# Second layer's convolution: taps read from the projection's PSUM bank, with the history columns written in front of it there

## The chip, the core and the metric

The kernel runs on one core of a Trainium2 chip. The metric is the device time of one execution in microseconds, and lower is better. The time before is the median of three runs. One more execution was taken with the hardware profiler, and its own time is given beside its span.

## What is computed

The reference is one inference step of a two-layer streaming encoder, for 1024 prompt frames of a new stream and 64 sample frames of a running one, with shared weights (1088 columns in all, model width 1024). Layer 0 mixes a gated short convolution with banded attention. Layer 1, which the change touches, is a gated DeltaNet of 8 heads. Cut to what matters:

```
def causal_dwconv(u, hist, w):            # width 4 in layer 1
    up = concatenate([hist, u], axis=1)   # 3 columns of history in front
    out = up[:, 0:T] * w[0]
    for j in range(1, 4):
        out = out + up[:, j:j + T] * w[j]
    return out, up[:, -3:]                # and the last 3 inputs, which are an output

def mixer_odd(h, conv_hist, S0, ...):
    p = h @ w_in                          # 1024 -> q | k | v | z | gates
    qkv, new_hist = causal_dwconv(p[q, k, v], conv_hist, conv_w)
    q, k, v = split(silu(qkv))            # 8 heads of 128
    S, o = gated_delta(l2norm(q), l2norm(k), v, g, beta, S0)   # chunks of 64 frames, one after the other
    y = (rmsnorm(o) * silu(z)) @ w_out
```

The prompt starts with a history of zeros, and the sample starts with three given columns.

## The kernel before

Everything is held with features on the 128 partitions and frames along the free dimension. The 1088 frames are cut into three groups, `GROUPS` (L22): 384, 384 and 320 columns. The third group holds the last 256 prompt columns and the 64 sample columns.

**Projection.** `project` (L172) computes one weight tile of 128 output features for one group: 24 matmuls (8 blocks of the contraction, each as three products of high and low parts) accumulate in one PSUM bank, a tile named `pjt` of 128 x 512 fp32 that `bank` (L126) hands out. Six banks serve at the start of layer 1; from its third group on, after `less_banks` (L136), there are two, which take turns. So a projection can begin only when nobody needs what the last but one left in its bank. The program's matmuls are all issued at L119 and its transposes at L124.

**Convolution.** `conv` (L699) takes the finished bank of one group and writes a slice of the tile `kq` (keys and queries of a head pair) or `vt` (values). Per group, ScalarE writes the fourth tap straight from PSUM into the destination (L713), and copies the bank into an SBUF tile `raw` behind three columns of history (L715). VectorE writes the history (L707, L710, L712). The first two taps are VectorE's scalar_tensor_tensor from `raw` (L719). The third is ScalarE's product into `tap` (L721), which GpSimd adds (L722). Then comes the SiLU (L729, or, for the six tiles of the first head pair, a tanh with a correction, L726 and L727). The third group is convolved in two pieces, prompt and sample. `raw` is handed to the next group as `prev`, whose last three columns are its history, and its tails go to HBM (L731, L732).

**Order of the work.** There are 24 such weight tiles, six for each of four head pairs. The first four of the first pair are projected group by group in the loop at L1143, with a small copy `tail` as history (L1163). The other 20 run through `conv_tile` (L735), the three groups of a tile one after the other. TensorE's order is fixed by the program: `Order` (L75) runs generators by rank, and the projection, of lowest rank, gives way after each pair of matmuls within a block; between the last matmul of one projection and the first two of the next nothing is put. Beside the projections run, for each pair and batch of chunks, `prepare` (L855), `substitute` (L918, a forward substitution on GpSimd, L930 and L931, with a trip through HBM on both sides), `join` (L938, which starts with GpSimd's L959 and VectorE's transpose `XT` at L960), `solve` (L1006), `scan` (L1032) and `finish` (L1104). The order on VectorE, ScalarE, GpSimd and the DMA queues is set by a scheduler when the program is built.

**Weights.** When a tile's three groups are done, `drop` (L168) stages another weight tile: ScalarE rounds the high part `whi` (L161) and VectorE subtracts for the low part `wlo` (L162), twice each. Both overwrite the buffer of a tile that was just used.

Of the kernel before, what the change touches and what calls it, by code (L numbers as in the profile page):

```python
# [7 lines left out]
F32 = mybir.dt.float32  # L8
F32R = mybir.dt.float32r
I32 = mybir.dt.int32  # L10
AF = mybir.ActivationFunctionType
ALU = mybir.AluOpType
# [3 lines left out]
P = 128  # L16
# [4 lines left out]
KT = D // P  # L21
GROUPS = ((0, 384), (384, 384), (768, 320))  # L22
GMAX = 384
# [29 lines left out]
P_SCC = 157  # L53
# [54 lines left out]
class Net:  # L108
# [60 lines left out]
        self.held -= 1  # L169
        self.ahead()  # L170

    def project(self, w, ops, n, m=P, ks=range(KT)):  # L172

        ps = self.bank()
        ks = list(ks)
        for k in ks:
            hi, lo = ops[0][k], ops[1][k]
            o = ps[0:m, :n]
            self.mm(o, w[0][:, k, :], hi, k == ks[0], False)
            self.mm(o, w[0][:, k, :], lo, False, False)  # L180
            yield 0
            self.mm(o, w[1][:, k, :], hi, False, k == ks[-1])
        return ps
# [484 lines left out]
    def odd(self):  # L668
        nc, tc, I, O = self.nc, self.tc, self.I, self.O
        act, dve, pool, par, cst = self.act, self.dve, self.pool, self.par, self.cst  # L670
        w_in, mix, order, Dd, od, Sd = I["w_in1"], self.mixd[1], self.order, self.Dd, self.od, self.Sd
        NB = len(BATCHES)
        k1 = self.open("k1")
# [22 lines left out]
        def ch(x):  # L696
            return x.rearrange("p (c t) -> p c t", t=64)

        def conv(ti, dst, g, ps, prev):  # L699
            t0, n = GROUPS[g]  # L700
            half = ti % 8 < 2
            cw = self.cwh[:, ti // 8, 4 * (ti % 8):4 * (ti % 8) + 4] if half else par[:, P_CWC + 4 * ti:P_CWC + 4 * ti + 4]
            cw = [cw[:, j:j + 1] for j in range(4)]
            pieces = [(0, 0, n)] if g < 2 else [(0, 0, 256), (259, 256, 64)]
            raw = k1.tile([P, GMAX + 3], F32, name="raw", tag="raw", bufs=3)
            if g == 0:
                dve.memset(raw[:, 0:3], 0.0)  # L707
            else:
                w = prev.shape[-1]
                dve.tensor_copy(raw[:, 0:3], prev[:, w - 3:w])  # L710
            if g == 2:
                dve.tensor_copy(raw[:, 259:262], par[:, P_SCC + 3 * ti:P_SCC + 3 * ti + 3])  # L712
            act.activation(dst[:, t0 // 64:(t0 + n) // 64, :], ch(ps[:, :n]), AF.Copy, scale=cw[3])  # L713
            for i0, off, m in pieces:
                act.copy(out=raw[:, i0 + 3:i0 + 3 + m], in_=ps[:, off:off + m])  # L715
            for i0, off, m in pieces:
                o = dst[:, (t0 + off) // 64:(t0 + off + m) // 64, :]
                for j in range(2):
                    dve.scalar_tensor_tensor(o, ch(raw[:, i0 + j:i0 + j + m]), cw[j], o, ALU.mult, ALU.add)  # L719
                t = k1.tile([P, GMAX + 3], F32, name="tap", tag="raw", bufs=3)[:, :m]  # L720
                act.activation(t, raw[:, i0 + 2:i0 + 2 + m], AF.Copy, scale=cw[2])  # L721
                pool.tensor_tensor(o, o, ch(t), ALU.add)  # L722
            o = dst[:, t0 // 64:(t0 + n) // 64, :]
            if half:
                th = k1.tile([P, GMAX + 3], F32, name="th", tag="raw", bufs=3)[:, :n]
                act.activation(ch(th), o, AF.Tanh)  # L726
                dve.scalar_tensor_tensor(o, ch(th), 1.0, o, ALU.add, ALU.mult)  # L727
            else:
                act.activation(o, o, AF.Silu)  # L729
            if g == 2:  # L730
                nc.scalar.dma_start(O["convC"][ti, 0], raw[:, 256:259])  # L731
                nc.scalar.dma_start(O["convC"][ti, 1], raw[:, 323:326])  # L732
            return raw

        def conv_tile(ti, dst):  # L735
            w = self.take()
            prev = None
            for g, (t0, n) in enumerate(GROUPS):
                ps = yield from self.project(w, self.hops(g), n)
                prev = conv(ti, dst, g, ps, prev)  # L740
            self.drop()

# [8 lines left out]
        def conv_dst(p, i):  # L751
            q = i % 2
            if i < 2:
                return 8 + 2 * p + q, KQ[p][:, 0, :, q, :]
            if i < 4:
                return 2 * p + q, KQ[p][:, 1, :, q, :]
            return 16 + 2 * p + q, V[p][:, :, q, :]
# [92 lines left out]
        def zeroed():  # L850
            for name, w in (("Cb", 32), ("BD", P)):
                Z[name] = self.kp.tile([P, NBM, w], F32, name=name)
                pool.memset(Z[name], 0.0)
# [287 lines left out]
        ws = [self.wba] + [self.take() for _ in range(WBUFS)] + [self.stage(self.queue.pop(0), k1, 0)]  # L1141
        prev = [None] * (WBUFS + 1)
        for g, (t0, n) in enumerate(GROUPS):  # L1143
            yield f"norm0{g}"
            if g == 2:
                self.close("opn")
                self.less_banks()
                self.pg = self.open("pg", space=PSUM)
                self.kp = self.open("k2", "right")
                zeroed()  # L1150
            for i in range(WBUFS + 2):
                if i == 0:
                    ps = yield from self.project(ws[0], self.hops(g), n, m=16)
                    act.copy(out=ba[:, t0:t0 + n], in_=ps[0:16, :n])
                    if g == 2:
                        order.add("gates", 2, gates(ba))
                        order.add("decays", 3, decays(), ["gates"])
                    continue
                ps = yield from self.project(ws[i], self.hops(g), n)
                raw = conv(*conv_dst(0, i - 1), g, ps, prev[i - 1])  # L1160
                if g < 2:
                    prev[i - 1] = k1.tile([P, 3], F32, name="tail", tag="tail", bufs=WBUFS + 2)
                    dve.tensor_copy(prev[i - 1], raw[:, GMAX:GMAX + 3])  # L1163
                elif i <= WBUFS:
                    self.drop()
        for p in range(4):
            if p > 1:
                yield f"scan{NB * (p - 2) + NB - 1}"
            if p:
                new_kq(p)  # L1170
            for i in range(WBUFS + 1 if p == 0 else 0, 6):
                if i == 4:
                    add_pair(p)
                    if p == 1:
                        yield "decays"
                    new_v(p)
                yield from conv_tile(*conv_dst(p, i))
            order.done.add(f"v{p}")
# [93 lines left out]
```

## Time and profile before

| what | value |
|---|---|
| three runs | 1504.11, 1497.92, 1495.92 us |
| median | 1497.92 us |
| the profiled execution's own time | 1498.51 us |
| its span, first to last instruction | 1496.7 us |
| matmul, busy | 1376.2 us (92%) |
| VectorE, busy | 858.7 us (57%) |
| ScalarE, busy | 745.6 us (50%) |
| GpSimd, busy | 402.1 us (27%) |
| granted TensorE clock, mean | 0.973 |

In the profile, PE is TensorE's matmul, PEld its weight load, DVE is VectorE, ACT ScalarE, POOL GpSimd and SP the DMA queue. A timeline row gives the start, the duration, the engine, the source line, the operation, out<-in with the shape, and how many were merged; in brackets stands the idle time of the engine just before and what ended it. Matmuls are pipelined, so a row's duration is longer than the distance to the next row. Layer 1's convolutions run from about 660 to 1216 us.

### The profile page before, as it was taken

Reading aid. Unit: us, or ns where it says so; the run is one execution under the profiler, and the core shown is the slowest. Engines: PE = TensorE matmul, PEld = TensorE weight load, DVE = VectorE, ACT = ScalarE, POOL = GpSimd, SP = SyncE. Lnnn points to the kernel's source line nnn. Section 1 sums busy time; section 2 is a strip of 40 time slices with the busy share of each in tenths; the row PEclk is TensorE's granted clock in tenths of the full one; section 3 lists DMA queues with packets and bytes.
Section 4 is the critical chain, followed back from the end, with each engine's and each line's share of the span. In section 5 each row is a group of like instructions: output and inputs, shape, how many; then the busy total and the mean of one; then the engine's idle time right before and its main releaser. Section 6 shows DMA issues by size and latency. Waiting matters only on the chain. (4 is left out here: it accounts for less than half of the span.)

```text
span 1496.7 us, 28755 instructions
## 1 busy us (share of the span) xinstructions
PE 1376.2 (92%) x10578; PEld 1237.4 (83%) x10578; DVE 858.7 (57%) x2400; ACT 745.6 (50%) x1948; POOL 402.1 (27%) x909
## 2 busy tenths in 40 slices
PE   4899999999999999898876999999989989999995
PEld 3888998999999899887765877778877778888985
DVE  6647237326525755776675667664756665443654
ACT  6544144235325456776655566556555644323642
POOL 4100000000000014432447254452645261410322
PEclk9999999999999999998987999999999999999998
DMA  5231210220211174541332112211211132337454
GB/s 201 83 114 44 77 58 26 87 65 29 74 61 58 44 233 149 180 146 36 94 87 63 31 51 57 42 41 47 67 35 41 37 96 60 99 108 238 154 190 156
DMA packets 114381, 133.15 MB, mean 89 GB/s; under 512 B 35568, under 2 KB 81336, under 8 KB 114240
## 3 DMA queue, kind: packets, MB, share of 16 engines
q1 hardware_dynamic: 82128, 101.86, 22.9%
q10 hardware_dynamic: 32112, 29.45, 6.1%
q8 instruction: 83, 1.36, 0.4%
q14 instruction: 58, 0.48, 0.1%
HBM read 99.91 MB, written 34.51 MB: 90 GB/s over the span
## 5 line engine op out<-in xcount | busy, mean ns | idle before, releaser
L119 PE MATMUL pjt<-hhi,wlo 128*128 128x384 f32 (+1 forms) x1768 | 621.4, 351 | 1.8 <-DVE wlo L162 1.8
L119 PE MATMUL pjt<-hhi,whi 128*128 128x384 f32 (+1 forms) x1768 | 587.5, 332 | 19.7 <-ACT ko L464 4.2
L119 PE MATMUL pjt<-hlo,whi 128*128 128x384 f32 (+1 forms) x1768 | 586.8, 332 | 7.3 <-DVE hlo L215 6.6
L119 PEld LDWEIGHTS pjt<-hhi,whi 128*128 128x128 f32 x1768 | 340.4, 193 | 29.1 <-ACT hhi L214 6.6
L119 PEld LDWEIGHTS pjt<-hhi,wlo 128*128 128x128 f32 x1768 | 340.3, 192 | 26.0 <-issue 12.2
L119 PEld LDWEIGHTS pjt<-hlo,whi 128*128 128x128 f32 x1768 | 339.0, 192 | 10.5 <-DVE hlo L215 8.8
L162 DVE TENSOR_TENSOR wlo<-wf,whi 128x512 fp32r<-128x512 f32 x222 | 155.6, 727 | 138.3 <-ACT whi L161 137.0
L161 ACT CAST whi<-wf 128x512 fp32r<-128x512 f32 x222 | 129.9, 619 | 154.7 <-PE pjt L119 110.9
L544 ACT ACTIVATE pr<-pr,mx 128x640 f32<-128x640 f32 (+5 forms) x72 | 50.9, 706 | 92.7 <-DVE mx L543 92.2
L722 POOL TENSOR_TENSOR kq<-kq,tap 128x384 f32<-128x384 f32 (+1 forms) x64 | 49.7, 784 | 140.5 <-DVE kq L719 99.5
L505 POOL MEMSET bias<- 64x64 f32 x8 | 1.5, 187 | 315.4 <-DMA bias<-Gd 245.0
L345 POOL TENSOR_TENSOR sqa<-sqa,sq 128x384 f32<-128x384 f32 (+1 forms) x36 | 39.7, 1103 | 150.1 <-ACT sq L343 150.0
L541 DVE CUSTOM_DVE_ANT_0 pr<-sc,bias 128x640 f32<-128x640 f32 (+5 forms) x72 | 48.0, 666 | 26.3 <-PE sc L119 22.8
L1093 DVE SCALAR_TENSOR_TENSOR S<-S,egl,su 128x128 f32<-128x128 f32 x128 | 41.1, 343 | 34.9 <-PE su L119 34.3
L930 POOL TENSOR_TENSOR px<-AL 48x14 f32<-48x14 f32 (+6 forms) x168 | 48.6, 289 | 40.0 <-DMA AL<-Sd 31.6
L931 POOL TENSOR_TENSOR AL<-AL,px 48x14 f32<-48x14 f32 (+6 forms) x168 | 52.4, 312 | 8.7
L719 DVE SCALAR_TENSOR_TENSOR kq<-raw,par,kq 128x384 f32<-128x384 f32 (+1 forms) x96 | 48.7, 526 | 9.9 <-ACT raw L715 9.7
L610 POOL TENSOR_TENSOR cvo<-cvo,th 128x384 f32<-128x384 f32 (+1 forms) x12 | 12.0, 999 | 142.6 <-DVE mx L543 113.3
L884 ACT ACTIVATE junk<-tr 128x128 f32<-128x128 f32 x136 | 38.0, 279 | 19.8 <-PE tr L124 16.5
L124 PE MATMUL pt<-cst,pr 128*128 128x128 f32 (+1 forms) x280 | 43.2, 270 | 4.4 <-DVE pr L546 2.9
L119 PE MATMUL pjt<-mhi,whi 128*128 128x384 f32 x128 | 43.5, 340 | 3.1 <-ACT mhi L161 3.1
L119 PE MATMUL pjt<-mlo,whi 128*128 128x384 f32 x128 | 43.7, 342 | 0.3 <-DVE mlo L162 0.3
(240 smaller groups left out, 2344.5 us busy)
## 6 DMA issues: line engine op xcount, KB each, us to landing
wf<-in_w_in SPq DMA_DIRECT2D x128, 256.0 KB, 3.2
wf<-in_w_out SPq DMA_DIRECT2D x96, 256.0 KB, 3.4
mf<-mixd SPq DMA_DIRECT2D x32, 192.0 KB, 3.5
x<-in_x SPq DMA_DIRECT2D x8, 384.0 KB, 5.3
xg<-in_x SPq DMA_DIRECT2D x2, 1536.0 KB
xd<-xg SPq DMA_DIRECT2D x2, 1536.0 KB, 6.9
Dd<-dbuf ACTq DMA_DIRECT2D x16, 192.0 KB, 2.2
od<-o ACTq DMA_DIRECT2D x12, 256.0 KB, 2.5
```

The costliest lines, as they stand in the source:

```text
L119: return self.pe.matmul(out, lhsT=lhsT, rhs=rhs, start=start, stop=stop, **k)
L124: return self.pe.transpose(out, in_, self.ident[0:k, 0:k])
L161: self.act.copy(out=hi, in_=x)
L162: (eng or self.dve).tensor_tensor(lo, x, hi.bitcast(F32), ALU.subtract)
L345: pool.tensor_tensor(acc, acc, sq, ALU.add)
L541: dve.tensor_tensor_reduce(out=cut(pr[0:nq, :nk]), in0=sc[0:nq, :nk // nw, :nw], in1=cut(b["bias"][a][0:nq, j0:j0 + nk]), scale=1.0, scala ...
L544: act.activation(pr[0:nq, :nk], pr[0:nq, :nk], AF.Exp, bias=mx[0:nq, 1:2], scale=1.0, accum_out=mx[0:nq, 2:3])
L719: dve.scalar_tensor_tensor(o, ch(raw[:, i0 + j:i0 + j + m]), cw[j], o, ALU.mult, ALU.add)
L722: pool.tensor_tensor(o, o, ch(t), ALU.add)
L930: pool.tensor_tensor(t, AL[:, j + 1:16, j:j + 1].broadcast_to([lanes, m, w]), x.broadcast_to([lanes, m, w]), ALU.mult)
L931: pool.tensor_tensor(o, o, t, ALU.add)
L1093: dve.scalar_tensor_tensor(Sn[:, q, :], S[:, q, :], egl[:, q, p, c:c + 1], su[q], ALU.mult, ALU.add)
```

## The change

The bank itself now holds the row of inputs. `project` gets an offset, so that layer 1's results stand in columns 4 onward of their bank. `conv` writes the three columns of history into columns 1 to 3 of the same bank and reads all four taps from there: the fourth by ScalarE as before, the other three by VectorE. The copy `raw`, ScalarE's product and GpSimd's addition are gone. For the sample piece VectorE writes the given history over the last three prompt columns in the bank, after the prompt's taps; before that, ScalarE saves both tails to a small tile `ends`, which goes to HBM. What the next group takes as history is now a slice of the bank, `ps[:, n + 1:n + 4]`. In the first loop it is copied to `tail` at once; in `conv_tile` it is read when the next group's `conv` runs.

```diff
-    def project(self, w, ops, n, m=P, ks=range(KT)):
+    def project(self, w, ops, n, m=P, ks=range(KT), off=0):
...
-            o = ps[0:m, :n]
+            o = ps[0:m, off:off + n]
...
-            raw = k1.tile([P, GMAX + 3], F32, name="raw", tag="raw", bufs=3)
+            o = dst[:, t0 // 64:(t0 + n) // 64, :]
+
+            act.activation(o, ch(ps[:, 4:4 + n]), AF.Copy, scale=cw[3])
+            if g == 2:
+                ends = k1.tile([P, 2, 3], F32, name="ends", tag="ends", bufs=3)
+                act.copy(out=ends, in_=ps[:, 257:385].rearrange("p (a b) -> p a b", b=64)[:, :, 0:3])
             if g == 0:
-                dve.memset(raw[:, 0:3], 0.0)
+                dve.memset(ps[:, 1:4], 0.0)
             else:
-                w = prev.shape[-1]
-                dve.tensor_copy(raw[:, 0:3], prev[:, w - 3:w])
-            if g == 2:
-                dve.tensor_copy(raw[:, 259:262], par[:, P_SCC + 3 * ti:P_SCC + 3 * ti + 3])
-            act.activation(dst[:, t0 // 64:(t0 + n) // 64, :], ch(ps[:, :n]), AF.Copy, scale=cw[3])
-            for i0, off, m in pieces:
-                act.copy(out=raw[:, i0 + 3:i0 + 3 + m], in_=ps[:, off:off + m])
-            for i0, off, m in pieces:
-                o = dst[:, (t0 + off) // 64:(t0 + off + m) // 64, :]
-                for j in range(2):
-                    dve.scalar_tensor_tensor(o, ch(raw[:, i0 + j:i0 + j + m]), cw[j], o, ALU.mult, ALU.add)
-                t = k1.tile([P, GMAX + 3], F32, name="tap", tag="raw", bufs=3)[:, :m]
-                act.activation(t, raw[:, i0 + 2:i0 + 2 + m], AF.Copy, scale=cw[2])
-                pool.tensor_tensor(o, o, ch(t), ALU.add)
-            o = dst[:, t0 // 64:(t0 + n) // 64, :]
+                dve.tensor_copy(ps[:, 1:4], prev)
+            for i0, m in [(0, n)] if g < 2 else [(0, 256), (256, 64)]:
+                if i0:
+                    dve.tensor_copy(ps[:, 257:260], par[:, P_SCC + 3 * ti:P_SCC + 3 * ti + 3])
+                oi = o[:, i0 // 64:(i0 + m) // 64, :]
+                for j in range(3):
+                    dve.scalar_tensor_tensor(oi, ch(ps[:, i0 + j + 1:i0 + j + 1 + m]), cw[j], oi, ALU.mult, ALU.add)
...
-            return raw
+            return ps[:, n + 1:n + 4]
...
-                ps = yield from self.project(w, self.hops(g), n)
+                ps = yield from self.project(w, self.hops(g), n, off=4)
                 prev = conv(ti, dst, g, ps, prev)
...
-                    dve.tensor_copy(prev[i - 1], raw[:, GMAX:GMAX + 3])
+                    dve.tensor_copy(prev[i - 1], last)
```

In the changed file the line numbers of the convolution are lower: the fourth tap is L706, `ends` L709, the history L711 (zeros), L713 (copy of `prev`) and L716 (sample), and the three taps L719. GpSimd's L930, L931 and L959 become L926, L927 and L955, and the transpose `XT` L956. TensorE's instructions stand in the same order in both programs; only what they wait for is other. On the other engines the scheduler has set a new order.

First, TensorE where one weight tile ends and the next begins, in `conv_tile`: the last matmuls of a third group (128x320) and the first of the next tile's first group (128x384), with the semaphores waited for. Before:

```order
L119 MATMUL pjt<-hhi_6901,wlo 128x320
L119 MATMUL pjt<-hhi_6901,whi 128x320
L119 MATMUL pjt<-hlo_6902,whi 128x320
L119 MATMUL pjt<-hhi_6901,wlo 128x320
L119 MATMUL pjt<-hhi_6035,whi 128x384 [waits Activation_49]
L119 MATMUL pjt<-hlo_6036,whi 128x384
L119 MATMUL pjt<-hhi_6035,wlo 128x384
```

And the same place of the changed kernel:

```order
L119 MATMUL pjt<-hhi_6885,wlo 128x320
L119 MATMUL pjt<-hhi_6885,whi 128x320
L119 MATMUL pjt<-hlo_6886,whi 128x320
L119 MATMUL pjt<-hhi_6885,wlo 128x320
L119 MATMUL pjt<-hhi_6035,whi 128x384 [waits DVE_49]
L119 MATMUL pjt<-hlo_6036,whi 128x384
L119 MATMUL pjt<-hhi_6035,wlo 128x384
```

The first matmul of the new projection waited for ScalarE, whose copy had emptied its bank one projection earlier; now it waits for VectorE, and by the semaphore's count for the copy of `prev` (L713) that belongs to the projection that ended one instruction ahead of it. The same holds where a tile's third group begins: 40 places in all, two for each of the 20 tiles of `conv_tile`.

Second, VectorE around the end of a third group, some 1012 us into the trace of before: the two subtractions for `wlo`, and what stands after them. Before:

```order
L682 TENSOR_SCALAR so<-so 128x2
L683 TENSOR_SCALAR so<-so 128x2
L162 TENSOR_TENSOR wlo<-wf,whi 128x512
L978 TENSOR_TENSOR XT<-XT,tr 128x5x16
L162 TENSOR_TENSOR wlo<-wf,whi 128x512
L979 STREAM_TRANSPOSE X<-XT 128x160
L1001 TENSOR_TENSOR BD<-XT,sT 32x5x32
```

And of the changed kernel:

```order
L682 TENSOR_SCALAR so<-so 128x2
L683 TENSOR_SCALAR so<-so 128x2
L162 TENSOR_TENSOR wlo<-wf,whi 128x512 x2
L713 COPY pjt<-pjt 128x3
L719 SCALAR_TENSOR_TENSOR kq<-pjt,par,kq 128x4x64 x3
L974 TENSOR_TENSOR XT<-XT,tr 128x5x16
L1108 SCALAR_TENSOR_TENSOR so<-so,rr 128x2
```

The copy of the history stands behind both subtractions, and the step of `join` that stood between them has moved behind the taps.

Third, VectorE around the first `XT` of the layer, the transpose that begins `join` (some 797 to 815 us in the trace of before). Before:

```order
L912 SCALAR_TENSOR_TENSOR Af<-An,cst,Af 128x96 x2
L719 SCALAR_TENSOR_TENSOR kq<-raw,par,kq 128x6x64
L710 COPY raw<-raw 128x3
L712 COPY raw<-par 128x3
L719 SCALAR_TENSOR_TENSOR kq<-raw,par,kq 128x6x64
L838 TENSOR_TENSOR dbuf<-tr,gc 128x320
L162 TENSOR_TENSOR wlo<-wf,whi 128x512 x2
L719 SCALAR_TENSOR_TENSOR kq<-raw,par,kq 128x4x64
L719 SCALAR_TENSOR_TENSOR kq<-raw,par,kq 128x64
L719 SCALAR_TENSOR_TENSOR kq<-raw,par,kq 128x4x64
L719 SCALAR_TENSOR_TENSOR kq<-raw,par,kq 128x64
L707 MEMSET raw 128x3
```

And of the changed kernel:

```order
L908 SCALAR_TENSOR_TENSOR Af<-An,cst,Af 128x96
L956 STREAM_TRANSPOSE XT<-X 128x192
L713 COPY pjt<-pjt 128x3
L908 SCALAR_TENSOR_TENSOR Af<-An,cst,Af 128x96
L719 SCALAR_TENSOR_TENSOR kq<-pjt,par,kq 128x6x64 x3
L834 TENSOR_TENSOR dbuf<-tr,gc 128x320
L162 TENSOR_TENSOR wlo<-wf,whi 128x512 x2
L713 COPY pjt<-pjt 128x3
L719 SCALAR_TENSOR_TENSOR kq<-pjt,par,kq 128x4x64 x3
```

Before, `XT` came right behind the last row shown, after the convolutions of this tile; now it stands ahead of the copy of the second group's history, for which TensorE's third group waits.

More of the change, by code (lines that the diff above doesn't have):

```diff
@@ L703, in conv @@
             cw = [cw[:, j:j + 1] for j in range(4)]
-            pieces = [(0, 0, n)] if g < 2 else [(0, 0, 256), (259, 256, 64)]
-            raw = k1.tile([P, GMAX + 3], F32, name="raw", tag="raw", bufs=3)
+            o = dst[:, t0 // 64:(t0 + n) // 64, :]
[3 more added lines that the diff above has]
+                act.copy(out=ends, in_=ps[:, 257:385].rearrange("p (a b) -> p a b", b=64)[:, :, 0:3])
             if g == 0:
-                dve.memset(raw[:, 0:3], 0.0)
+                dve.memset(ps[:, 1:4], 0.0)
             else:
-                w = prev.shape[-1]
-                dve.tensor_copy(raw[:, 0:3], prev[:, w - 3:w])
-            if g == 2:
-                dve.tensor_copy(raw[:, 259:262], par[:, P_SCC + 3 * ti:P_SCC + 3 * ti + 3])
-            act.activation(dst[:, t0 // 64:(t0 + n) // 64, :], ch(ps[:, :n]), AF.Copy, scale=cw[3])
-            for i0, off, m in pieces:
-                act.copy(out=raw[:, i0 + 3:i0 + 3 + m], in_=ps[:, off:off + m])
-            for i0, off, m in pieces:
-                o = dst[:, (t0 + off) // 64:(t0 + off + m) // 64, :]
-                for j in range(2):
-                    dve.scalar_tensor_tensor(o, ch(raw[:, i0 + j:i0 + j + m]), cw[j], o, ALU.mult, ALU.add)
-                t = k1.tile([P, GMAX + 3], F32, name="tap", tag="raw", bufs=3)[:, :m]
-                act.activation(t, raw[:, i0 + 2:i0 + 2 + m], AF.Copy, scale=cw[2])
-                pool.tensor_tensor(o, o, ch(t), ALU.add)
-            o = dst[:, t0 // 64:(t0 + n) // 64, :]
+                dve.tensor_copy(ps[:, 1:4], prev)
[5 more added lines that the diff above has]
+                    dve.scalar_tensor_tensor(oi, ch(ps[:, i0 + j + 1:i0 + j + 1 + m]), cw[j], oi, ALU.mult, ALU.add)
             if half:
@@ L730, in conv @@
             if g == 2:
-                nc.scalar.dma_start(O["convC"][ti, 0], raw[:, 256:259])
-                nc.scalar.dma_start(O["convC"][ti, 1], raw[:, 323:326])
-            return raw
+                for a in range(2):
+                    nc.scalar.dma_start(O["convC"][ti, a], ends[:, a, :])
+            return ps[:, n + 1:n + 4]
         def conv_tile(ti, dst):
@@ L1158, in odd @@
                     continue
-                ps = yield from self.project(ws[i], self.hops(g), n)
-                raw = conv(*conv_dst(0, i - 1), g, ps, prev[i - 1])
+                ps = yield from self.project(ws[i], self.hops(g), n, off=4)
+                last = conv(*conv_dst(0, i - 1), g, ps, prev[i - 1])
                 if g < 2:
                     prev[i - 1] = k1.tile([P, 3], F32, name="tail", tag="tail", bufs=WBUFS + 2)
-                    dve.tensor_copy(prev[i - 1], raw[:, GMAX:GMAX + 3])
+                    dve.tensor_copy(prev[i - 1], last)
                 elif i <= WBUFS:
```

## The prediction

> **What bounds the kernel now.** I read the page first, then the busy time by stretches, then TensorE's waits in the stretch that the change touches, and last the timeline at the places where one projection follows another. Two lines of the page:
>
> ```profile
> span 1496.7 us, 28755 instructions
> PE 1376.2 (92%) x10578; PEld 1237.4 (83%) x10578; DVE 858.7 (57%) x2400; ACT 745.6 (50%) x1948; POOL 402.1 (27%) x909
> ```
>
> TensorE is busy for 92% of the span, so the question is where it will stand still. The next rows give, for three stretches from 740 to 1230 us (the 20 tiles of `conv_tile`), the busy time of PE, PEld, DVE, ACT and POOL, then the granted clock, the DMA's share and GB/s:
>
> ```profile
> 740.00:815.00 75.00, 49.46 (x279) 42.68 (x281) 52.94 (x125) 44.43 (x124) 42.55 (x67) 0.86 0.33 85
> 815.00:1210.00 395.00, 375.56 (x3791) 313.24 (x3791) 245.04 (x914) 225.50 (x741) 178.43 (x526) 0.98 0.19 47
> 1210.00:1230.00 20.00, 13.75 (x166) 12.59 (x166) 12.45 (x45) 7.18 (x20) 16.06 (x55) 0.83 0.33 83
> ```
>
> From 815 to 1210 us TensorE is busy 95% of the time and VectorE 62%; ahead of it and behind it the chain of the DeltaNet's preparation makes TensorE wait. Its waits from 740 to 1230 us, by who ended them (total, times, longest):
>
> ```profile
> PE tr L119 <- DVE XT L960: 12.2, 3, 9.3
> PE tr L124 <- DVE o L1114: 7.2, 3, 5.3
> ...
> PE tr L119 <- DVE XT L978: 0.2, 1, 0.2
> ```
>
> There are 18 such rows, 51.2 us in sum, and none is a wait of a projection for its bank: a bank was emptied by ScalarE soon after its projection's end, with a whole projection's time to spare. ScalarE, VectorE and GpSimd hold TensorE up through the preparation's chain alone.
>
> **What the change takes away** lies off that path.
>
> ```profile
> L722 POOL TENSOR_TENSOR kq<-kq,tap 128x384 f32<-128x384 f32 (+1 forms) x64 | 49.7, 784 | 140.5 <-DVE kq L719 99.5 <-DVE so L1108 14.8 <-DVE so L1109 9.0
> L722 POOL TENSOR_TENSOR vt<-vt,tap 128x384 f32<-128x384 f32 (+2 forms) x32 | 24.5, 769 | 48.3 <-DVE vt L719 25.9 <-DVE rt L687 8.4 <-ACT qs L1081 6.3
> L719 DVE SCALAR_TENSOR_TENSOR kq<-raw,par,kq 128x384 f32<-128x384 f32 (+1 forms) x96 | 48.7, 526 | 9.9 <-ACT raw L715 9.7
> ```
>
> GpSimd loses 96 additions, 49.7 + 24.5 = 74 us, and with them its waits for VectorE's taps; ScalarE loses the copy and the product. VectorE gains one tap for each of 96 pieces, 96 x 0.526 = 50 us. Five sixths of them, 42 us, fall from 740 to 1230 us, where it is busy for 53 + 245 + 12 = 310 of 490 us: 72% with them, still not the bound. A tap that reads PSUM costs no more: a scalar_tensor_tensor with an operand in PSUM takes
>
> ```profile
> L480 DVE SCALAR_TENSOR_TENSOR zb<-th,pjt x12: 480/554/555, 81.3 to 466.6; 128x384 f32<-128x384 f32 x8, 128x320 f32<-128x320 f32 x4
> ```
>
> 0.554 us at the median. I count all this at nothing directly; what GpSimd's freedom does for TensorE's waits stands below.
>
> **What it adds: 40 waits of TensorE.** The bank of a group is now kept for the next group's history, and that copy stands in the next group's `conv`, behind ScalarE's fourth tap, which waits for the next projection's last matmul. With two banks the projection after that needs the very bank that is kept. So at the start of each third group, and of each next tile's first group, TensorE stands from its last matmul through ScalarE's tap and VectorE's copy. Queued behind the waiting matmul is everything of the scan and the preparation that TensorE was to do next. [...] The trace of before has each part of that handover, first at the start of a third group:
>
> ```profile
> 1026.25 0.34 PE L119 MATMUL pjt<-hhi,wlo 128*128 128x384 f32 x1
> ...
> 1026.42 0.31 PE L119 MATMUL pjt<-hhi,whi 128*128 128x320 f32 x1
> ...
> 1026.62 0.58 ACT L713 ACTIVATE kq<-pjt,par 128x384 f32<-128x384 f32 x1 [0.43 <-PE pjt L119]
> ...
> 1028.31 0.16 DVE L710 COPY raw<-raw 128x3 f32<-128x3 f32 x1
> ```
>
> The last matmul ends at 1026.59, ScalarE starts 0.03 later and is done at 1027.20. With 0.16 for VectorE's copy and 0.03 at each of two more handovers TensorE goes on at 1027.42 in place of 1026.42: 1.0 us lost. 20 x 1.0 = **20 us**. At the start of the next tile it is more, because the weight buffer falls free at the same moment:
>
> ```profile
> 1011.03 0.31 PE L119 MATMUL pjt<-hhi,wlo 128*128 128x320 f32 x1
> ...
> 1011.18 0.34 PE L119 MATMUL pjt<-hhi,whi 128*128 128x384 f32 x1
> ...
> 1011.23 1.14 ACT L161 CAST whi<-wf 128x512 fp32r<-128x512 f32 x2 [0.17 <-PE pjt L119]
> ...
> 1011.89 0.69 DVE L162 TENSOR_TENSOR wlo<-wf,whi 128x512 fp32r<-128x512 f32 x1
> ...
> 1012.28 0.52 ACT L713 ACTIVATE kq<-pjt,par 128x320 f32<-128x320 f32 x1
> ...
> 1012.64 0.69 DVE L162 TENSOR_TENSOR wlo<-wf,whi 128x512 fp32r<-128x512 f32 x1
> ```
>
> ScalarE does both casts ahead of the tap, and in the new order VectorE does both subtractions ahead of the copy. The second subtraction ended at 1013.33; the step between them (0.23) has moved behind, so take 1013.1. With copy and handovers TensorE goes on at about 1013.35 in place of 1011.18: 2.2 us. 20 x 2.2 = **44 us**. Neither price was seen as a wait; the floor is the shorter handover at all 40 (40 us), and the ceiling is 3 us where VectorE is in arrears, 20 + 60 = 80.
>
> **Places where the copy stands behind `XT`.** At the first one TensorE now stops where the third group begins:
>
> ```profile
> 796.89 0.32 PE L119 MATMUL pjt<-hhi,whi 128*128 128x320 f32 x1
> ...
> 814.95 0.84 PE L119 MATMUL tr<-XT,Cb 32*32 32x16 f32 x48 [9.30 <-DVE XT L960]
> ...
> 814.52 0.38 DVE L960 STREAM_TRANSPOSE XT<-X 128x192 f32<-128x192 f32 x1 [6.57 <-POOL X L959]
> ```
>
> Before, it worked from 796.89 to 805.65 and then stood 9.30 us. Now those 8.8 us of work come after `XT`. GpSimd, without three or four additions of 0.78 us in the chain, should bring `XT` some 3 us sooner: net 6. Elsewhere:
>
> ```profile
> 927.46 0.31 PE L119 MATMUL pjt<-hhi,whi 128*128 128x320 f32 x1
> ...
> 934.83 0.38 DVE L960 STREAM_TRANSPOSE XT<-X 128x192 f32<-128x192 f32 x1 [1.33 <-POOL X L959]
> ...
> 1213.81 0.31 PE L119 MATMUL pjt<-hhi,wlo 128*128 128x320 f32 x1
> 1220.76 1.09 PE L124 MATMUL tr<-cst,o 128*128 128x128 f32 x4 [5.25 <-DVE o L1114]
> ...
> 1226.88 0.38 DVE L960 STREAM_TRANSPOSE XT<-X 128x192 f32<-128x192 f32 x1 [2.57 <-POOL X L959]
> ```
>
> At 927.46 `XT` comes 7.4 us later; 1.0 is counted, some 2 go by GpSimd's freedom and about 1 by the pause before it: 3.5. At the last boundary, 1214.1, it comes 13 us later, of which 5.25 were waited anyway: net 7. Together **17 us**, between 5 and 30.
>
> **What is swallowed.** While TensorE pauses, the others catch up. Of the 51.2 us of old waits the two long ones (9.3 and 5.3) are used above; 36.6 remain, and I take two thirds as gone: **-24 us**, between 0 and -37.
>
> **The clock.** A pause can cost more than itself:
>
> ```profile
> 1059.94 0.63 PE L124 MATMUL tr<-cst,kq 128*128 128x128 f32 x4 [2.12 <-DVE KQD L906]
> 1060.73:1064.14 3.41, 3.41 (x13) 3.41 (x12) 3.18 (x13) 3.28 (x12) 2.28 (x12) 0.50 0.51 134
> 1064.14:1067.55 3.41, 3.41 (x24) 3.36 (x23) 0.94 (x5) 2.16 (x11) 0.60 (x3) 1.00 0.08 15
> 795.47 0.88 PE L119 MATMUL tr<-dbuf,cst 128*128 128x384 f32 x2 [2.64 <-DVE KQD L906]
> 795.47:798.88 3.41, 3.41 (x20) 3.15 (x21) 3.34 (x9) 1.43 (x4) 3.08 (x7) 1.00 0.33 96
> ```
>
> After a pause of 2.12 us the clock was 0.50 for 3.41 us, in which 13 matmuls ran in place of 24: 3.41 x 11/24 = 1.56 us lost. After one of 2.64 us it stayed at 1.00. I take half of the 20 longer pauses: 10 x 1.56 = **16 us**, between 0 and 20 + 8 such drops (44). [...]
>
> **First four tiles.** Their history is copied at once, so a bank is held through its own six taps only. A third group's taps take 3 x 0.48 (L480's least, 320 columns) and three short ones, with ScalarE ahead: about as long as the next projection of 24 x 0.15 = 3.6 us. I take **3 us**, between 0 and 8.
>
> **Sum.** 20 + 44 + 17 - 24 + 16 + 3 = 76 us, made against the profiled execution's 1498.5 us (span 1496.7 and 1.8 around it), which lies 0.6 above the median of the runs: 1574.5, so **1575 us**.
>
> **Rivals.** (1) All terms but the clock's: 1498.5 + 60 = 1559, if pauses of 2.2 us are too short to lower it, as the one of 2.64 us at 795.47 was. [...] (2) The pauses lie just where TensorE would have waited for the chain anyway: 20 + 44 + 17 + 3 - 51 = +33, 1531. Against it: from 815 to 1210 us TensorE idles 19.4 us in all, and 33 of the 40 pauses lie there. (3) VectorE is in arrears at each new tile (80 in place of 64), few old waits vanish (-10), and the clock falls after all long pauses (44): 80 + 20 - 10 + 44 + 3 = +137, 1635. (4) Faster: VectorE's copies are early enough that the pauses vanish among the others' waits, and GpSimd, 74 us lighter, takes away the waits at `XT` and `o` (12.2 + 7.2): 1498.5 - 19 = 1479. It decides only if a boundary costs under about 0.4 us, less than ScalarE's tap of 0.58 alone; I see no row for it. (5) Nothing changes: the pauses and the swallowed waits come out even, 64 and 17 against 51 and a lighter GpSimd; the idle 19.4 us speak against it too.
>
> **How the numbers follow.** The forecast has 0.48, rival (1) 0.22, (2) 0.15, (3) 0.10, (4) 0.03, (5) 0.02. The range from 1528 to 1620 takes in the first three and, one or two at a time, the bounds of the terms (all the low ends at once would give 1506, all the high ones 1660); it leaves out the upper half of (3) and a tail of (2). About 0.5% (7.5 us) is what a measurement of this kernel can tell from no change. Slower by more: 0.95; within it: 0.02; faster: 0.03.
>
> **What would show it.** In the profile of the changed kernel, TensorE's waits should have a row for `pjt` released by VectorE's copy at L713, 40 times, near 1.0 us at the third groups and 2.2 at new tiles, with a few of 5 to 14 us. GpSimd's busy time should fall by about 74 us, VectorE's rise by about 50, and the clock from 740 to 1230 us be lower. If that row is missing or short, the prediction is wrong at its root; if it is there and the time is near 1530, the swallowed part is; if the clock column hasn't moved, rival (1) holds.

## The result and the profile after

The changed kernel takes **1544.1 us** at the median of four runs (1540.33 to 1546.06); four runs of the kernel before took 1496.9 at the median. The ratio is 1.0304, with a 95% interval from 1.0261 to 1.0347: slower by 45.6 us of the 1498.5 that the prediction counted from, where it had 76.

| | before | after |
|---|---|---|
| span of the profiled execution | 1496.7 us | 1540.5 us |
| matmul, busy | 1376.2 us | 1395.9 us |
| VectorE, busy | 858.7 us | 887.1 us |
| ScalarE, busy | 745.6 us | 682.7 us |
| GpSimd, busy | 402.1 us | 316.1 us |
| granted clock, mean | 0.973 | 0.968 |

Of the prediction's other signs, GpSimd's busy time fell by 86 us (about 74 expected), VectorE's rose by only 28 (about 50 expected), and the mean clock fell.

The first row of TensorE's waits of the whole changed kernel (total, times, longest) is the one that the prediction asked for:

```profile
PE pjt L119 <- DVE pjt L713: 63.8, 40, 3.1
```

Forty waits, 63.8 us. The longest, of 3.1, is not one of the 40 places but belongs to the first loop, and one of the 40 is put down to L1104, the instruction behind the copy. The 20 at starts of third groups sum to 21.4 us, the 20 at next tiles to 40.9 with that one. Next the rows behind it in the stretch from 740 to 1280 us, where the 20 tiles of `conv_tile` now lie:

```profile
PE tr L119 <- DVE KQD L902: 5.7, 4, 4.9
PE tr L119 <- ACT junk L880: 2.5, 2, 1.9
PE pjt L119 <- DVE so L1104: 1.6, 1, 1.6
...
PE tr L124 <- DVE dbuf L834: 0.2, 1, 0.2
```

There are eight of them, 13.0 us in sum, with the one of L1104. Before, the waits for the preparation's chain made 51.2 us, headed by `XT` with 12.2. The row for `XT` is gone.

Then a start of a third group, in the timeline:

```profile
1017.52 0.34 PE L119 MATMUL pjt<-hhi,wlo 128*128 128x384 f32 x1
...
1017.90 0.58 ACT L706 ACTIVATE kq<-pjt,par 128x384 f32<-128x384 f32 x1 [2.05 <-PE pjt L119]
...
1018.51 0.17 DVE L713 COPY pjt<-pjt 128x3 f32<-128x3 f32 x1 [1.38 <-ACT kq L706]
...
1018.73 0.42 PE L119 MATMUL pjt<-hhi,whi 128*128 128x320 f32 x1 [0.87 <-DVE pjt L713]
```

The four steps follow each other as forecast: last matmul, ScalarE's tap, VectorE's copy, next matmul. The idle time of 0.87 us is what it is at most of these places. And a start of the next tile:

```profile
1024.99 0.31 PE L119 MATMUL pjt<-hhi,wlo 128*128 128x320 f32 x1
...
1025.19 1.14 ACT L161 CAST whi<-wf 128x512 fp32r<-128x512 f32 x2 [0.17 <-PE pjt L119]
...
1025.85 1.29 DVE L162 TENSOR_TENSOR wlo<-wf,whi 128x512 fp32r<-128x512 f32 x2
...
1026.24 0.52 ACT L706 ACTIVATE kq<-pjt,par 128x320 f32<-128x320 f32 x1
...
1027.06 0.16 DVE L713 COPY pjt<-pjt 128x3 f32<-128x3 f32 x1
...
1027.28 0.44 PE L119 MATMUL pjt<-hhi,whi 128*128 128x384 f32 x1 [1.97 <-DVE pjt L713]
```

Both casts are done ahead of the tap, then tap and `ends`, then the copy: 1.97 us idle. At the first place where the copy stands behind `XT`, the prediction counted 6 us of loss (8.8 less some 3):

```profile
793.33 0.65 POOL L955 TENSOR_TENSOR X<-Xf,cst 128x96 f32<-128x96 f32 x2 [1.86 <-DMA Xf<-Sd]
...
795.22 0.37 DVE L956 STREAM_TRANSPOSE XT<-X 128x192 f32<-128x192 f32 x1
795.51 0.14 DVE L713 COPY pjt<-pjt 128x3 f32<-128x3 f32 x1
...
795.71 0.63 PE L119 MATMUL pjt<-hhi,whi 128*128 128x320 f32 x1 [1.32 <-DVE pjt L713]
```

`XT` is there 19 us sooner than before (it started at 814.52), and the pause is 1.32 us.

For the comparisons below I use a ledger of two entries, each the difference between two profiled executions. **Waits** is the sum of all rows of TensorE's waits in the whole span (before 107.6 us, after 130.7). **Clock** is worked out from the mean clock: a time of span x (1 - clock) x 2 at half speed (the clock records of before and after hold 1.00 and 0.50 alone), and 1.56 us lost for each 3.41 us of it, as the prediction worked out. What neither shows (short gaps, matmul spans that are modelled) is the rest, up to 15 us here; between the kernel before and the changed one it is 12.6 of the 43.8 us of span.

### The profile page after: what moved, and what is told of

Read it like the earlier page. It is cut to its first block, busy times and chain, and to the rows that moved or that the text cites. A ratio compares the mean times of both kernels' runs of the same rounds, so it can differ in the third digit from the quotient of the medians.

```text
span 1540.5 us, 28409 instructions
## 1 busy us (share of the span) xinstructions
PE 1395.9 (91%) x10578; PEld 1247.1 (81%) x10578; DVE 887.1 (58%) x2496; ACT 682.7 (44%) x1780; POOL 316.1 (21%) x813
## 5 line engine op out<-in xcount | busy, mean ns | idle before, releaser
L119 PE MATMUL pjt<-hhi,whi 128*128 128x384 f32 (+1 forms) x1768 | 595.6, 337 | 83.0 <-DVE pjt L713 63.8
L162 DVE TENSOR_TENSOR wlo<-wf,whi 128x512 fp32r<-128x512 f32 x222 | 154.4, 724 | 147.2 <-ACT whi L161 145.4
L719 DVE SCALAR_TENSOR_TENSOR kq<-pjt,par,kq 128x384 f32<-128x384 f32 (+2 forms) x144 | 71.8, 499 | 3.5
L541 DVE CUSTOM_DVE_ANT_0 pr<-sc,bias 128x640 f32<-128x640 f32 (+5 forms) x72 | 48.0, 666 | 26.3 <-PE sc L119 22.8
L926 POOL TENSOR_TENSOR px<-AL 48x14 f32<-48x14 f32 (+6 forms) x168 | 46.1, 274 | 64.3 <-DMA AL<-Sd 55.0
L690 POOL TENSOR_TENSOR so<-so 128x4 f32<-128x4 f32 (+2 forms) x72 | 15.9, 221 | 199.7 <-DVE so L683 132.2
L1048 ACT ACTIVATE junk<-o 128x128 f32<-128x128 f32 x68 | 21.0, 309 | 80.2 <-DVE o L1044 65.3
L927 POOL TENSOR_TENSOR AL<-AL,px 48x14 f32<-48x14 f32 (+6 forms) x168 | 46.7, 278 | 9.8
```

What stands on the lines that cost most here:

```text
L119: return self.pe.matmul(out, lhsT=lhsT, rhs=rhs, start=start, stop=stop, **k)
L162: (eng or self.dve).tensor_tensor(lo, x, hi.bitcast(F32), ALU.subtract)
L541: dve.tensor_tensor_reduce(out=cut(pr[0:nq, :nk]), in0=sc[0:nq, :nk // nw, :nw], in1=cut(b["bias"][a][0:nq, j0:j0 + nk]), scale=1.0, scala ...
L719: dve.scalar_tensor_tensor(oi, ch(ps[:, i0 + j + 1:i0 + j + 1 + m]), cw[j], oi, ALU.mult, ALU.add)
L926: pool.tensor_tensor(t, AL[:, j + 1:16, j:j + 1].broadcast_to([lanes, m, w]), x.broadcast_to([lanes, m, w]), ALU.mult)
L927: pool.tensor_tensor(o, o, t, ALU.add)
```

## The experiments

All kernels leave TensorE's order of work as it is; on the other engines each has its own order, set by the scheduler. A ratio is to runs of the kernel before that were made beside the kernel's own (medians 1496.9 to 1501.5 us), with its 95% interval; spans are those of single profiled executions.

| kernel | median, us | ratio | span | clock | waits |
|---|---|---|---|---|---|
| after | 1544.1 | 1.0304 (1.0261 to 1.0347) | 1540.5 | 0.968 | 130.7 |
| tail copied at once | 1484.1 | 0.9908 (0.9883 to 0.9933) | 1481.9 | 0.976 | 93.8 |
| tail at once, first group only | 1523.9 | 1.0149 (1.0113 to 1.0184) | 1522.0 | 0.964 | 113.2 |
| tail at once, second group only | 1502.5 | 1.0015 (1.0000 to 1.0031) | 1500.5 | 0.974 | 105.3 |
| copy ahead of the tap | 1486.1 | 0.9911 (0.9891 to 0.9930) | 1483.7 | 0.983 | 93.4 |
| before, third tap on VectorE | 1490.5 | 0.9934 (0.9915 to 0.9953) | 1489.3 | 0.975 | 99.7 |
| tail at once, third tap as before | 1503.2 | 1.0018 (1.0001 to 1.0034) | 1505.6 | 0.974 | 111.5 |
| after, third tap as before | 1574.9 | 1.0494 (1.0473 to 1.0515) | 1572.4 | 0.957 | 151.9 |
| after, two reads more | 1590.4 | 1.0592 (1.0568 to 1.0616) | 1590.3 | 0.949 | 153.4 |
| after, one read more | 1551.9 | 1.0322 (1.0273 to 1.0371) | 1550.1 | 0.966 | 138.2 |
| tail at once, unused additions | 1495.5 | 0.9954 (0.9933 to 0.9974) | 1492.3 | 0.980 | 105.7 |
| after, unused additions | 1568.6 | 1.0435 (1.0410 to 1.0461) | 1563.3 | 0.964 | 148.7 |
| tail at once, copy ahead of the tap | 1477.3 | 0.9822 (0.9795 to 0.9849) | 1476.4 | 0.978 | 88.7 |

**Is it the kept bank?** The history is copied out of the bank behind the group's taps, in `conv_tile`:

```diff
                 prev = conv(ti, dst, g, ps, prev)
+                if g < 2:
+                    last, prev = prev, k1.tile([P, 3], F32, name="tail", tag="tail", bufs=WBUFS + 2)
+                    dve.tensor_copy(prev, last)
```

> The changed kernel, but in conv_tile the last three columns of a group are copied to a small SBUF tile right behind its taps (one more VectorE copy for the first and second group of a tile), as the first loop does already; nothing else differs. Theory A (the kept bank is the cause): the 40 waits of pjt for L713, 63.8 us, are gone, the old waits for the preparation chain come back, and the time is about that of the kernel before, 1497 us, or up to 15 us below it if a lighter GpSimd shortens that chain: 1482 to 1500. Theory B (the waits only show a VectorE that is overloaded by 50 us of taps from PSUM, or taps that are slower there): projections go on waiting for VectorE, and at most half of the 46 us comes back: 1520 to 1544.

Measured: 1484.1 us. The span is 58.6 us shorter than the changed kernel's, with 40 copies more on VectorE. So the pauses that the kept bank makes are the whole of the loss, and an overloaded VectorE is out. Without the pauses the change is a gain: 14.8 us of span against the kernel before (waits -13.8, clock -4.4). Rows from the top of its waits:

```profile
PE tr L124 <- DVE KQD L905: 6.8, 4, 4.0
PE tr L119 <- DVE KQD L905: 6.7, 5, 5.6
...
PE tr L124 <- DVE o L1113: 4.6, 1, 4.6
```

The chain's waits are back, but `XT`'s is only 0.7 us.

**What each kind of pause costs.** The same copy under `g == 0` takes away the 20 pauses at third groups, under `g == 1` the 20 at the next tile.

> The same copy for the first group of a tile alone, so that only the 20 pauses at the start of third groups go (about 19 of the 63.8 us). By the prediction's price of 1.0 us each, with no clock drop, the time falls by about 20: 1524 us. If pauses are mostly swallowed by waits that would come anyway, it falls by less than 10: 1534 or more. If even short pauses cost clock, by more than 30: 1514 or less.

> The same copy for the second group alone, so that only the 20 pauses at the start of the next tile go (about 45 of the 63.8 us). By the prediction's terms, 44 for the pauses and 11 to 16 for the clock behind them, less some of the old waits (up to 24) that return: a fall of 31 to 60, 1484 to 1513 us. If the outer pauses are not the bank's but the weight split's (its casts and subtractions end late whichever bank is free), the wait moves to the split's row and the time falls by less than 10: over 1534.

Measured: 1523.9 and 1502.5 us. The waits that are left, first of the one with only the pauses at the next tile (one row more than these 20 comes from the first loop), then of the one with only those at third groups:

```profile
PE pjt L119 <- DVE pjt L713: 45.8, 21, 4.3
```

```profile
PE pjt L119 <- DVE pjt L713: 25.3, 21, 3.1
```

The spans close as a square. The pauses at third groups cost 18.5 us (1540.5 - 1522.0) or 18.6 (1500.5 - 1481.9), those at the next tile 40.0 or 40.1. That it closes to 0.1 us is luck: four runs of the first of these kernels lie between 1512.9 and 1530.9. By the ratios the two ways give 23 or 16 us, and 43 or 36. So no effect of the two on each other is seen, but one of some 7 us could hide. At third groups it is 0.93 us each, close to their idle time. At the next tile it is 2.0 each, and not simply their wait: against the kernel without pauses the waits grow by only 19.4 us in all, since some 22 us of the others are swallowed, but the half-speed time grows from 71 to 110 us, 17.6 us of loss.

**Is it ScalarE's tap in the handover?** The kept banks stay, and the copy goes ahead of the tap:

```diff
+            if g:
+                dve.tensor_copy(ps[:, 1:4], prev)
             act.activation(o, ch(ps[:, 4:4 + n]), AF.Copy, scale=cw[3])
...
-            else:
-                dve.tensor_copy(ps[:, 1:4], prev)
```

> The changed kernel with the history copy put ahead of ScalarE's fourth tap, so that the copy waits for the projection's last matmul alone and the tap for the copy; the banks are kept as in the changed kernel. Theory A: the 40 waits stay, but an inner pause shrinks by the tap of 0.58 us and a handover, to about 0.3 to 0.4 us; the outer ones shrink little, as both subtractions of the split stand ahead of the copy on VectorE and follow both casts of ScalarE: by 0 to 0.3 us each. The wait's row falls from 63.8 to about 48, the time by 10 to 18: 1526 to 1534. Theory B (load of VectorE): no change, 1540 to 1548.

Measured: 1486.1 us, far better than expected. A start of the next tile shows why:

```profile
1000.66 0.31 PE L119 MATMUL pjt<-hhi,wlo 128*128 128x320 f32 x1
...
1000.86 1.14 ACT L161 CAST whi<-wf 128x512 fp32r<-128x512 f32 x2 [0.17 <-PE pjt L119]
...
1001.08 0.16 DVE L707 COPY pjt<-pjt 128x3 f32<-128x3 f32 x1
...
1001.38 0.41 PE L119 MATMUL pjt<-hhi,whi 128*128 128x384 f32 x1 [0.41 <-DVE so L682]
...
1001.51 1.29 DVE L162 TENSOR_TENSOR wlo<-wf,whi 128x512 fp32r<-128x512 f32 x2
```

I had expected both subtractions to stay ahead of the copy. But in the new order the copy stands ahead of them, presumably because it needs only the last matmul and is ready earlier, so the pause of 1.97 us became one of 0.41 here (the profile puts it down to the instruction behind the copy). The row of this kernel's waits:

```profile
PE pjt L119 <- DVE pjt L707: 19.0, 34, 2.5
```

The bank is still kept through a whole projection; what cost time was the length of the handover. The half-speed time is the least of all (50 us).

**Where the gain without pauses comes from.** First the kernel before, with the third tap on VectorE from `raw`, without ScalarE's product and GpSimd's addition:

```diff
-                for j in range(2):
+                for j in range(3):
                     dve.scalar_tensor_tensor(o, ch(raw[:, i0 + j:i0 + j + m]), cw[j], o, ALU.mult, ALU.add)
-                t = k1.tile([P, GMAX + 3], F32, name="tap", tag="raw", bufs=3)[:, :m]
-                act.activation(t, raw[:, i0 + 2:i0 + 2 + m], AF.Copy, scale=cw[2])
-                pool.tensor_tensor(o, o, ch(t), ALU.add)
```

> The kernel before (SBUF copy kept, banks released by ScalarE), with the third tap done by VectorE as in the changed kernel: GpSimd's 96 additions and ScalarE's 96 products are gone. Theory A (the changed kernel without its pauses is 14 us faster than the kernel before because GpSimd, freed, no longer holds up the chain at XT and o): a gain of 10 to 16 us, 1482 to 1490, and the row of waits for XT (12.2 us) nearly gone. Rival (the 14 us come from the SBUF copy that ScalarE and VectorE are spared): at most 4 us of gain, 1494 to 1500.

Measured: 0.9934, 10 us faster, at the edge of what was expected. The wait for `XT` is halved, not gone (12.2 before):

```profile
PE tr L119 <- DVE XT L957: 6.5, 1, 6.5
```

Then the opposite, the version with the tail at once and the third tap as before (`range(2)`, product from the bank, addition on GpSimd):

> The version with the tail copied at once (no kept banks), but the third tap as before: ScalarE's product, read from PSUM, and GpSimd's addition. By theory A the gain of 14 us over the kernel before goes again: 1494 to 1502 us, and waits for XT return. By the rival (the SBUF copy) it stays: 1482 to 1488.

Measured: 1503.2 us; the gain is gone, but not by `XT`, which is in no row of over 1.6 us. The new row is the bank's:

```profile
PE pjt L119 <- ACT tap L721: 19.3, 10, 6.0
```

ScalarE's product reads the bank late, and projections wait for it. So this run mixed two things. The next one parts them: the additions alone, on a sum that nobody uses, with all taps still VectorE's.

```diff
                 for j in range(3):
                     dve.scalar_tensor_tensor(oi, ch(ps[:, i0 + j + 1:i0 + j + 1 + m]), cw[j], oi, ALU.mult, ALU.add)
+                t = k1.tile([P, GMAX + 3], F32, name="tap", tag="raw", bufs=3)[:, :m]
+                pool.tensor_tensor(ch(t), oi, oi, ALU.add)
```

> The version with the tail copied at once, all taps on VectorE, and one addition on GpSimd for each of the 96 pieces whose sum nobody uses (it reads the piece after its taps, so the activation waits for it as it did before). ScalarE gets no product back and no bank waits for GpSimd. If GpSimd's additions by themselves hold up the preparation's chain: 1493 to 1500 us, with longer waits for XT or o. If the loss of the version with the pool kept (1503 against 1484) came from ScalarE's product out of the bank, this one stays at 1482 to 1488.

Measured: 1495.5 us, and 10.4 us of span more than without them. `XT` is back:

```profile
PE tr L119 <- DVE XT L961: 5.6, 1, 5.6
```

So GpSimd's additions are worth 7 to 10 us, taken out (there with ScalarE's product) or put in. That GpSimd's work slows VectorE's instructions is not seen: VectorE's subtraction at L162 takes 0.727 us with the additions (before) and 0.722 without (third tap on VectorE). GpSimd's product `kt` in `prepare` shows that GpSimd is ahead without them (busy, mean ns, idle time just before it); the rows are those of the kernel before, of the one with the tail at once, and of the one with the unused additions:

```profile
L896 POOL TENSOR_TENSOR kt<-kt,kap 128x768 f32<-128x768 f32 (+1 forms) x12 | 17.2, 1437 | 12.7 <-DVE sA L894 9.9 <-DVE kap L895 2.7
```

```profile
L895 POOL TENSOR_TENSOR kt<-kt,kap 128x768 f32<-128x768 f32 (+1 forms) x12 | 16.8, 1403 | 63.8 <-DVE sA L893 39.2 <-PE pjt L119 21.9 <-DVE kap L894 2.7
```

```profile
L897 POOL TENSOR_TENSOR kt<-kt,kap 128x768 f32<-128x768 f32 (+1 forms) x12 | 16.9, 1407 | 11.2 <-DVE sA L895 7.1 <-DVE kap L896 3.7 <-PE pjt L119 0.3
```

With the additions GpSimd waits about 1 us for the operands of each `kt` (12.7 and 11.2 us over 12), without them 5 us (63.8): it is there earlier. Among the steps of the substitution, though, no addition waits. In the kernel before additions stand there in ten of the twelve substitutions, with 19.4 us of work and no wait of over 0.1 us, as here (L930 and L931 are the steps):

```profile
789.01 0.60 POOL L930 TENSOR_TENSOR px<-AL 48x54 f32<-48x54 f32 x1
789.61 1.00 POOL L722 TENSOR_TENSOR kq<-kq,tap 128x384 f32<-128x384 f32 x1
790.57 1.00 POOL L841 TENSOR_TENSOR dbuf<-cst,dbuf 128x384 f32<-128x384 f32 x1
791.53 0.29 POOL L931 TENSOR_TENSOR AL<-AL,px 48x54 f32<-48x54 f32 x1
```

The idle time of 140.5 + 48.3 us ahead of the 96 additions lies outside of the substitutions; whether it delays the work that leads up to them is not shown.

**Why the 17 us at `XT` failed.** The changed kernel with its kept banks and the third tap as before, and then with the unused additions alone:

> The changed kernel with its kept banks, but the third tap as before: ScalarE's product, from PSUM, and GpSimd's addition. It asks whether the prediction's 17 us at XT failed because GpSimd was freed. Theory A: XT comes late again, the copy stands behind it, and pauses of 5 us and more appear in the row of pjt waiting for L713: 1556 to 1575 us. Rival (the 17 us failed because the pauses themselves let the chain catch up): the row's longest pause stays near 3 us and the time is 1540 to 1552.

> The changed kernel with the same unused additions on GpSimd. It asks what made the changed kernel with the third tap on ScalarE and GpSimd 31 us slower. If GpSimd's additions: 1562 to 1578 us, with pauses of over 4 us behind L713 at places where XT is late. If ScalarE's product: 1542 to 1550. Between them, by the 10 us that the kernel before gained without the additions: 1554.

Measured: 1574.9 and 1568.6 us. With GpSimd's load put back, the changed kernel is at the time that was forecast for it, and the rival (the pauses alone let the chain catch up) is out as the whole of it. Their rows:

```profile
PE pjt L119 <- DVE pjt L713: 64.7, 38, 4.7
...
PE pjt L119 <- ACT tap L721: 8.4, 2, 6.0
```

```profile
PE pjt L119 <- DVE pjt L713: 75.8, 41, 5.2
```

The time came as theory A said, its picture only in part. With the unused additions 12.0 of the 22.8 us of span are in the pauses' row; the waits in all grow by 18.0 and the clock's loss by 6.4. With the third tap as before no pause in the row of L713 reached 5 us; of its 31.9 us, 8.4 are the bank read late by ScalarE and 16.8 the clock.

Each of the two has two pauses of over 4 us in that row, and only one of the two stands behind `XT` (4.56 us in the first kernel; 4.20 in the second, where `XT` starts at 809.06 and the matmul at 810.16). The other came by a way that neither the prediction nor the expectation had. Here it is in the first kernel:

```profile
1136.71 0.21 POOL L929 TENSOR_TENSOR px<-AL 48x14 f32<-48x14 f32 x1 [6.23 <-DMA AL<-Sd]
...
1136.93 0.98 POOL L722 TENSOR_TENSOR kq<-kq,tap 128x384 f32<-128x384 f32 x1
...
1137.95 0.52 ACT L728 ACTIVATE kq<-kq 128x384 f32<-128x384 f32 x1 [3.27 <-POOL kq L722]
...
1138.38 0.56 ACT L706 ACTIVATE kq<-pjt,par 128x384 f32<-128x384 f32 x1
...
1138.97 0.17 DVE L713 COPY pjt<-pjt 128x3 f32<-128x3 f32 x1 [4.91 <-ACT kq L706]
...
1139.19 0.64 PE L119 MATMUL pjt<-hhi,whi 128*128 128x320 f32 x1 [4.73 <-DVE pjt L713]
```

The addition stands behind the first step of a substitution, which waits for its data; ScalarE's SiLU waits for the addition, ScalarE's tap stands behind the SiLU, and VectorE's copy and TensorE wait for the tap. With the unused additions the pause of 5.2 us came the same way: there the SiLU waited 3.48 us for GpSimd, with the casts and the tap behind it. So the same additions that cost 10.4 us of span where no bank is kept cost 22.8 where the handover is on TensorE's path.

**The clock.** Two more reads of the bank ahead of the tap, and then one, make the pauses at third groups longer:

```diff
+            if hold and g == 1:
+                x = k1.tile([P, GMAX + 3], F32, name="xx", tag="raw", bufs=3)[:, :n]
+                for _ in range(2):
+                    act.copy(out=x, in_=ps[:, 4:4 + n])
             act.activation(o, ch(ps[:, 4:4 + n]), AF.Copy, scale=cw[3])
```

`hold` is set in `conv_tile` alone; the second version has no loop.

> The changed kernel with two more reads of the bank by ScalarE (about 0.43 us each, to a tile that nobody uses) ahead of the fourth tap of every second group, so that the 20 pauses at the start of third groups grow from 0.9 to about 1.8 us, near the 2.1 of the outer ones. If all of it is on the path and the clock falls only behind longer pauses: +18 us, 1562. If pauses of 1.8 us lower the clock as the outer ones do (11 more windows of half clock by 1.56 us): +30 to +36, 1574 to 1580. If the pauses are mostly swallowed by the chain's own waits: under +9, below 1553.

> The changed kernel with one more read of the bank by ScalarE in place of two, so that the 20 pauses at the start of third groups are about 1.3 us (0.87 in the changed kernel, 1.77 with two reads). The pauses alone add 20 x 0.45 = 9 us: 1553. If the loss of clock grows evenly with the pause, half of the 15 windows of half clock that two reads added: 1565. If pauses of 1.3 us already lower it as those of 1.8 do: 1573 to 1580. If the clock falls only from some length over 1.3 us: 1550 to 1556, with 75 to 90 us of half clock from 600 to 1300 us.

Measured: 1590.4 and 1551.9 us, with pauses at third groups of 1.77 and 1.26 us at the median in place of 0.87. The rows of two reads and of one:

```profile
PE pjt L119 <- DVE pjt L717: 84.5, 41, 3.3
```

```profile
PE pjt L119 <- DVE pjt L716: 71.9, 40, 3.1
```

One read adds 8.1 us to this row and 9.6 to the span; the half-speed time is 105 us in place of 99, and 75 us of it lie from 600 to 1300 us (78.5 in the changed kernel). The four runs of this kernel lie between 1542 and 1560 us, so its 9.6 us are less sure than the row. Two reads add 20.7 to the row and 49.8 to the span; the half-speed time goes to 162 us, 19 windows of 3.41 us more, which is 29 us. This is more than any of the three cases expected. So somewhere between 1.26 and 1.77 us these pauses begin to cost clearly more than themselves.

**Does a version beat both?** The tail at once and the copy ahead of the tap:

> Both remedies together: the tail copied at once, so that no bank is kept, and the history copied in ahead of ScalarE's tap. If the 18 us of short waits that the version with the copy first still had are on the path: 1466 to 1474 us. If they only stood in the place of the chain's own waits, as 20 of the 64 us in the changed kernel did: 1480 to 1487, no better than either. If the tap's new wait for VectorE hurts where no bank is kept: 1488 or more.

Measured: 0.9822 (0.9795 to 0.9849), the fastest of all, 1.8% under the kernel before. That lies between the first two cases: some of the 18 us of short waits was on the path, not all. No wait for the history's copy is left among TensorE's, and their sum is the least (88.7 us).

## Why the prediction came out as it did

Slower was right, and so was the main cause; the sum was 30 us too high (76 against 45.6). By its terms:

- **Pauses of 1.0 us at third groups, 20 us:** right. 0.87 us idle at most of them, 21.4 us in sum, and 18.5 us by the spans.
- **Pauses of 2.2 us at the next tile, 44 us; the clock, 16 us; swallowed, -24 us:** right in sum and nearly in each. Idle 1.97 us at the place shown, 2.0 at the median, 40.9 in sum; half-speed time 27.5 us more than without pauses, 8 windows and 12.6 us; the waits other than for `pjt`'s history fall from 89.0 to 66.9 us, 22 us. That the last two came so near is partly luck: half of the pauses and two thirds of the old waits were choices that no row fixed. Together with the first term the prediction has 56 us for the kept bank, the spans 58.6, of which the ledger leaves some 9 unexplained.
- **Places behind `XT`, 17 us, and "I count all this at nothing directly":** the step that failed. The prediction had `XT` come some 3 us sooner at the first place and 2 at the second; at the first it came 19 us sooner, the pauses at the three places are 1.3, 1.6 and 2.8 us, and the forecast pauses of 5 to 14 us did not come. So apart from the bank the change gains 14.8 us of span where the sum had a loss of 20 (17 at `XT` and 3 at the first four tiles). These 35 us, less the 2.6 by which the bank was priced too low, are the 32 us of the miss by the spans. The time lies inside the forecast's range, but this term lies outside its own bounds of 5 to 30. GpSimd's additions have a main part in it: put back unused, they bring 14 of the 19 us at the first place back (`XT` at 809.06; 795.22 in the changed kernel), and they account for 7 to 10 of the 14.8.

  How they do it is shown only in part. The 3 us were right for the additions alone: 3.0 us of them stand among the steps of the first substitution, and taken out of the kernel before they bring `XT` 3.1 us sooner (811.39). In the changed kernel that substitution also starts 6.3 us sooner, takes 13.3 us in place of 21.9, with neither additions nor `kt` among its steps, and its result is back from HBM 3.8 us after its last step in place of 9.4. Which of these follows from the lighter GpSimd and which from the scheduler's new order stays open; the copy and product that ScalarE is spared were not tried alone.
- **Rivals.** The first (no clock term, 1559) had the wrong reason: the clock did fall, to 0.968 from the 0.976 of the version without pauses. The second (all old waits swallowed, 1531) was off in the other direction: 22 us were swallowed and not 51. The third (VectorE in arrears) is out by the pauses of 2.0 us at the median, and the fifth (no change) by the ratio. The fourth was right that a lighter GpSimd takes away the wait for `XT`, and wrong that it could outweigh the pauses.

## What to carry to other kernels

Here a result that stayed in its PSUM bank until the next step read it made that read a part of TensorE's path: 40 waits, 63.8 us. With two banks, copy out the few columns that are needed, at once (1484.1 us in place of 1544.1), or put that copy ahead of everything else that waits for the same matmul (1486.1). The price of work on an engine whose order is fixed depends on what stands behind it: the same 96 additions cost 10.4 us in one version and 22.8 in another, so follow whose instruction waits for theirs before calling them free. Here a pause of TensorE cost about its own length up to 1.26 us; the 20 of 1.77 us at the median cost 29 us of clock besides. Of the changed kernel's pauses of 1.7 to 2.3 us that began at full clock between 740 and 1290 us, 8 of the 9 that lay inside one window of the grid below were followed by a window at half clock, and 3 of the 7 that lay across a border of two.

## What the runs showed of the hardware

In all fourteen traces the drops of the granted clock between 100 and 1400 us lie at multiples of 3.413 us from each other, to within some 2 ns. The traces cut along their grid from 740 to 1300 us give windows that can be sorted by TensorE's busy share. Of those at full clock, under 0.4, all 74 were followed by a window at half clock; from 0.4 to 0.5, 48 of 61; from 0.5 to 0.6, 31 of 77; from 0.6 to 0.7, 4 of 88; at 0.7 and more, none of 1768. In the traces of before and after alone these are 13 of 13, 7 of 10, 2 of 8, none of 14 and none of 249. Two places of the changed kernel show it (the columns are those of the prediction's stretches; PE first, the clock third from the end). A pause of 1.97 us inside one window:

```profile
854.69:858.11 3.42, 3.42 (x28) 2.66 (x27) 2.13 (x11) 1.14 (x4) 0.39 (x3) 1.00 0.16 24
858.11:861.52 3.41, 1.44 (x10) 0.91 (x9) 2.60 (x6) 1.62 (x4) 3.33 (x14) 1.00 0.20 54
861.52:864.93 3.41, 3.41 (x15) 2.65 (x15) 2.12 (x11) 0.00 (x0) 3.24 (x15) 0.50 0.31 101
```

And one of the same length that lies across a border of two:

```profile
960.51:963.92 3.41, 1.79 (x14) 1.52 (x12) 1.08 (x2) 1.99 (x5) 0.00 (x0) 1.00 0.00 0
963.92:967.33 3.41, 3.06 (x19) 2.51 (x19) 3.10 (x11) 0.81 (x5) 0.00 (x0) 1.00 0.55 157
```

Busy for 1.44 of 3.41 us, the next window is at 0.50; busy for 1.79, it is not. So by these counts a pause of 0.87 us, which leaves 0.75 of a window, did not lower the clock alone; one of 1.26 leaves 0.63, where 4 of 88 did; and one of 1.8 to 2.0 inside a window leaves 0.41 to 0.47, where 48 of 61 did. This also tells apart the prediction's two pauses of 2.12 and 2.64 us, with and without a drop: on the grid of that trace the first lies inside the window from 1057.32 to 1060.73 us, with TensorE busy for 1.29 of 3.41, and the second lies across the border at 794.49, with 1.75 busy ahead of it and 2.43 behind.
